# Moving the gather and combination steps of an expert pair out of the w1/w3 products and next to the transposes, in a one-core MoE kernel

## The chip, the cores and the metric

The kernel runs on one core of one Trainium2 chip. The metric is the device time in microseconds (us) of one execution; lower is better.

## The reference, cut to what matters

One encoder block: a mixer (two convolution and state-space branches, not touched here), then a mixture of experts on 512 tokens of width 1024. Each token goes to its two best experts of 64. Everything is float32.

```python
def expert_block(args):
    xblk, e = args
    hdn = jax.nn.silu(xblk @ w1[e]) * (xblk @ w3[e])   # 1024 -> 512
    return hdn @ w2[e]                                  # 512 -> 1024
...
return jnp.zeros_like(xt).at[buf_tok].add(yb * buf_w[:, None])
...
h = h + g2 * moe.reshape(bsz, seq, d)
return _rmsnorm(h, final_g)
```

The tokens of an expert are gathered, go through three weight matrices of 2 MB each, are scaled by their routing weight and are added back to the rows of h that they came from.

## The kernel before

The second half of the program runs over 32 pairs p of experts, two experts e = 0, 1 in a pair, with up to 64 tokens each. The order of instructions is the order of the Python code; TensorE (PE) takes them one after the other, and so do VectorE (DVE), ScalarE (ACT), GpSimd (POOL) and the DMA queue of SyncE (SP).

For one expert, TensorE does:

- `hidden`: the w1 and w3 products, written `ps_w`, for k = 0 to 7, each k with four recorded matmuls of 64 columns of weights (32 in all). ScalarE then applies Silu (tile `sl`) and VectorE multiplies the two halves.
- `hidden_t`: two transposes into `ps_ht`; VectorE copies them out (tile `ht`).
- `second`: the w2 product, written `ps_y`, 16 recorded matmuls of 64 columns of weights.

Two generators supply work for neighbouring pairs, and both use all 128 columns of weights:

- `gather`, letter g: 8 steps a pair, each 12 bf16 matmuls into `ps_g`. They pick the tokens of the *next* pair. After step 4 and after step 8, ScalarE turns what was gathered into four slices each of `xg`, the input of the next pair's `hidden`.
- `combine`, letter c: 8 steps a pair, which add the results of the *previous* pair to h. A step is two matmuls, from `yh` and `yl`, into one `ps_o` tile, and one VectorE addition `h<-h,ps_o` that empties it. The tiles `ps_o` come from the pool `po_` (line 1225), which has two buffers, used in turn: a step can't write before the addition of the step before last has read its buffer.

Between an expert's instructions stand ten places, numbered 0 to 9: 0 to 7 ahead of each k of `hidden`, 8 between `hidden` and the transposes, 9 between the transposes and `second`. A table says which letters stand in which place; `FILL` (line 1375) is that of pairs 3 to 30, 28 pairs, with one row for e = 0 and one for e = 1. What is left of c and g when a pair is done is taken behind `second` of e = 1. Then VectorE builds the one-hot tiles `S` of a later gather (`choose`), and `scale_y` makes `y`, `yh`, `yl` and `so` out of `ps_y` for the next pair's c.

The weights come through a ring of eight 2 MB buffers, named `wb`, whose loads SyncE issues as the products release them.

Of the kernel before, what the change touches and what calls it, by code (L numbers as in the profile page):

```python
# [128 lines left out]
def hybrid_block(ctx: ExitStack, tc: tile.TileContext, a, out, dbg=None, stage=9):  # L129
# [1207 lines left out]
    def combine(ys):  # L1337

        for c in range(4):
            for x in range(2):  # L1340
                yh, yl, st = ys[x][:3]
                if c in sums:
                    ps = sums[c][:, x * T:(x + 1) * T]
                else:
                    ps = pw.tile([P, T], F32, name="ps_o", tag="w") if sums else po_.tile([P, T], F32, name="ps_o", tag="o")
                PE.matmul(ps, lhsT=st[:, c * P:(c + 1) * P], rhs=yh, start=c not in sums, stop=False)
                PE.matmul(ps, lhsT=st[:, c * P:(c + 1) * P], rhs=yl, start=False, stop=True)
                if c not in sums:
                    hv = h[:, c, x * T:(x + 1) * T]
                    V.tensor_add(hv, hv, ps)  # L1350
                yield

    def to_psum():

        pp.close()
        pf = me.enter_context(tc.tile_pool(name="pf", bufs=1, space=PSUM, reuse_waits="tile"))
        for c in range(2):
            ps = pf.tile([P, D], F32, name=f"ps_f{c}", tag=f"f{c}")
            for x in range(2):
                q = slice(x * T, (x + 1) * T)  # L1360
                PE.matmul(ps[:, q], lhsT=ident, rhs=h[:, c, q], start=True, stop=False)
                yield
            sums[c] = ps

    def yps_():
        return [pyy.tile([P, T], F32, name=f"ps_y{x}", tag=f"y{x}") for x in range(2)]
# [5 lines left out]
    FILL1 = [v.split(",") for v in ",,,,g,g,g,g,gg,gg;cx,xc,xc,xc,xc,xc,xc,xc,xc,".split(";")]  # L1372
    FILL2 = [v.split(",") for v in "x,x,x,x,c,c,c,,c,;c,g,gc,g,gc,g,gc,g,g,gc".split(";")]
    FILL3 = [v.split(",") for v in ",c,c,c,c,c,c,c,,;c,,,,,,,,z,z".split(";")]
    FILL = [v.split(",") for v in ",,,,cgcc,,,,gg,gc;,,cgcc,,,,,,gg,gc".split(";")]

    def steps(gen, n):
        for _ in range(n):
# [83 lines left out]
    for p in range(npair):  # L1462
        yps, fl_ = yps_(), FILL3 if p == npair - 1 else (FILL0, FILL1, FILL2, FILL)[min(p, 3)]
        more = {"c": combine(pend) if pend else tb, "g": iter(()), "x": sp_, "G": g0, "z": to_psum()}
# [231 lines left out]
```

## Time and profile before

| | |
|---|---|
| time, median of 3 runs | 1854.08 us (1853.91 to 1859.2) |
| the profiled execution's own time | 1856.45 us |
| its span in the trace | 1854.7 us |
| TensorE busy | 1758.9 us, 95% of the span |
| VectorE busy | 1086.1 us, 59% |
| ScalarE busy | 540.1 us, 29% |
| GpSimd busy | 417.6 us, 23% |
| HBM read | 502.98 MB |

The page gives each engine's busy time over the whole span. Stages have different limits, so the shares alone don't say what a stage waits for; for that the trace is asked for the time of a stage, the waits in it, and the instructions in order of time.

### The profile page before, as it was taken

The numbers are of one execution on the slowest core, as the hardware profiler recorded it, in microseconds if no ns is written. First come the engines' busy times: TensorE is split into PE (matmuls) and PEld (weight loads), VectorE is DVE, ScalarE is ACT, GpSimd is POOL, SyncE is SP. The second block draws the span as 40 slices with busy tenths as digits, with TensorE's granted clock in tenths as the row PEclk, the third lists the DMA queues.
The fourth block names the chain that finished last, engine by engine and source line by source line (L and its number), as shares of the span: only waits on it lengthen the run. The fifth ranks groups of instructions, "written<-read, shape, count | busy, mean of one in ns | idle before, by whom it ended". The sixth has DMA issues, their size and how long they took to land.

```text
span 1854.7 us, 25500 instructions
## 1 busy us (share of the span) xinstructions
PE 1758.9 (95%) x10188; PEld 1048.2 (57%) x10188; DVE 1086.1 (59%) x1728; ACT 540.1 (29%) x901; POOL 417.6 (23%) x288
## 2 busy tenths in 40 slices
PE   5999989989899989999999999999999999999996
PEld 2676767767677878853444444444444444444442
DVE  6789999999989476344334343434343343434344
ACT  2443535425444553433111111111111111111112
POOL 3123341534415454312011111101010101011111
PEclk7999999999999989999999999999999999999998
DMA  6252422524235657568899999999999999999971
GB/s 254 72 162 60 138 89 79 159 69 135 96 111 159 231 203 252 218 247 317 344 386 407 390 406 403 396 405 392 407 389 407 392 405 392 406 389 405 395 319 46
DMA packets 97561, 506.91 MB, mean 273 GB/s; under 512 B 10208, under 2 KB 14560, under 8 KB 51616
## 3 DMA queue, kind: packets, MB, share of 16 engines
q1 hardware_dynamic: 97440, 505.25, 71.0%
q8 instruction: 82, 1.34, 0.3%
q14 instruction: 39, 0.32, 0.1%
HBM read 502.98 MB, written 2.23 MB: 272 GB/s over the span
## 4 chain that ended last, share of the span: by engine, by line
PE 75%; DVE 16%; issue 4%; ACT 2%; DMA 1%; POOL 0%; SPq 0%; DVEq 0%; ACTq 0%; POOLq 0%
PE ps_w L124 24%; PE ps_y L124 13%; PE ps_mm L124 12%; PE ps_g L124 10%; PE ps_o L124 7%; DVE accv L124 4%; DVE w_lo L124 3%; PE ps_cv L124 2%; PE ps_mix L124 2%; PE ps_ys L124 2%; DVE mE L124 2%; DVE ct L124 2%; DVE xs L124 1%; PE ps_ht L124 1%; PE ps_ada L124 1%
## 5 line engine op out<-in xcount | busy, mean ns | idle before, releaser
L124 PE MATMUL ps_w<-wb,xg 128*64 128x512 f32 x2048 | 470.7, 597 | 0.0
L124 DVE TENSOR_TENSOR h<-h,ps_o 128x512 f32<-128x512 f32 x252 | 167.9, 686 | 286.1 <-PE ps_o L124 286.1
L124 PEld LDWEIGHTS ps_w<-wb,xg 128*64 128x64 f32 x2048 | 138.7, 137 | 268.1 <-issue 265.8
L124 PE MATMUL ps_y<-wb,ht 128*64 128x512 f32 x1024 | 236.5, 604 | 2.5 <-DVE ht L124 2.5
L124 PE MATMUL ps_mm<-n1h,w_lo 128*128 128x512 f32 x560 | 224.7, 401 | 10.7 <-DVE w_lo L124 10.7
L124 PE MATMUL ps_mm<-n1h,w_hi 128*128 128x512 f32 x560 | 230.1, 411 | 0.2 <-ACT w_hi L216 0.2
L124 PE MATMUL ps_mm<-n1l,w_hi 128*128 128x512 f32 x560 | 223.2, 398 | 0.0
L124 PE MATMUL ps_g<-S,hg 128*128 128x128 bf16 (+1 forms) x2976 | 210.5, 223 | 1.5 <-DVE S L124 1.5
L124 DVE SCALAR_TENSOR_TENSOR accv<-u,par,accv 128x511 f32<-128x511 f32 (+29 forms) x240 | 206.0, 900 | 6.1 <-ACT accv L437 4.2
L1329 POOL TENSOR_SCALAR so<-par,tabA 128x512 fp32r<-128x512 f32 x32 | 50.0, 1563 | 690.1 <-PE ps_o L124 659.3
L124 PEld LDWEIGHTS <-hg 128*128 128x128 bf16 x2784 | 160.4, 98 | 67.7 <-issue 67.0
L1298 ACT ACTIVATE sl<-ps_w 128x256 f32<-128x256 f32 x64 | 24.6, 384 | 595.5 <-PE ps_w L124 595.5
L124 DVE TENSOR_TENSOR sl<-sl,ps_w 128x256 f32<-128x256 f32 x64 | 39.0, 609 | 259.1 <-ACT sl L1298 259.1
L124 DVE TENSOR_TENSOR w_lo<-w_raw,w_hi 128x1024 fp32r<-128x1024 f32 (+1 forms) x103 | 137.3, 1333 | 81.3 <-ACT w_hi L216 74.0
L216 ACT CAST w_hi<-w_raw 128x1024 fp32r<-128x1024 f32 (+1 forms) x103 | 107.2, 1041 | 266.7 <-PE ps_mm L124 102.7
L124 PEld LDWEIGHTS ps_y<-wb,ht 128*64 128x64 f32 x1024 | 68.6, 138 | 136.8 <-issue 131.2
L1286 ACT ACTIVATE xg<-ps_g,cB,cG 128x128 f32<-128x128 f32 x256 | 96.4, 457 | 144.7 <-PE ps_g L124 144.7
L124 PEld LDWEIGHTS ps_mm<-n1h,w_lo 128*128 128x128 f32 x560 | 108.1, 193 | 39.3 <-DVE w_lo L124 16.0
L124 PEld LDWEIGHTS ps_mm<-n1h,w_hi 128*128 128x128 f32 x560 | 108.2, 193 | 25.9 <-issue 2.4
L124 PEld LDWEIGHTS ps_mm<-n1l,w_hi 128*128 128x128 f32 x560 | 108.6, 194 | 24.4 <-issue 2.2
L124 PE MATMUL ps_o<-yh,so 128*128 128x512 f32 x252 | 117.1, 465 | 2.0 <-DVE h L124 1.3
L844 POOL TENSOR_TENSOR ada_acc<-ada_acc,ada_w 128x512 f32<-128x512 f32 x56 | 89.9, 1607 | 110.6 <-ACT ada_w L842 108.7
(325 smaller groups left out, 2173.2 us busy)
## 6 DMA issues: line engine op xcount, KB each, us to landing
wb<-in_w_dram SPq DMA_DIRECT2D x244, 1024.0 KB, 8.2
wb<-in_w_dram SPq DMA_DIRECT2D x57, 2048.0 KB, 10.0
w_raw<-in_w_in_dram SPq DMA_DIRECT2D x72, 512.0 KB, 3.6
wb<-in_w_dram SPq DMA_DIRECT2D x52, 512.0 KB, 6.9
ada_w<-in_w_ada_dram SPq DMA_DIRECT2D x64, 256.0 KB, 3.6
ada_w<-in_w_ada_dram SPq DMA_DIRECT2D x16, 512.0 KB, 9.1
mE<-sdram SPq DMA_DIRECT2D x32, 256.0 KB, 6.2
w_raw<-in_w_ssm_dram SPq DMA_DIRECT2D x16, 512.0 KB, 3.5
```

What stands on the lines that cost most here:

```text
L124: return f(*args, **kw)
L216: S.copy(hi[:, :n], raw[:, :n])
L844: G.tensor_add(acc, acc, w)
L1286: S.activation(xg[:, q], ps[:, i], AF.Identity, bias=cB2[:, q:q + 1], scale=cG2[:, q:q + 1])
L1298: S.activation(sl, ps[:, 0], AF.Silu)
L1329: G.tensor_scalar(st, tok, tabs2[x][0], None, op0=OP.is_equal)
```

## The change

One line, the table `FILL` of pairs 3 to 30:

```diff
-    FILL = [v.split(",") for v in ",,,,cgcc,,,,gg,gc;,,cgcc,,,,,,gg,gc".split(";")]
+    FILL = [v.split(",") for v in ",,,,,,,,ggc,gccc;,,,,,,,,ggc,gccc".split(";")]
```

Place 4 (e = 0) and place 2 (e = 1) held c g c c and are now empty. Place 8 held g g and holds g g c; place 9 held g c and holds g c c c. That is four c for each expert as before, but three g in place of four: the last two g of a pair go to its end, behind `second` of e = 1.

TensorE in pair 3, e = 0, between the transposes and the w2 product. `ps_o<-yh` and `ps_o<-yl` are one combination step; "waits DVE" marks a matmul that waits for VectorE. Before:

```order
L124 LDWEIGHTS hg
L124 MATMUL ps_g<-S,hg 128x128
L124 MATMUL ps_o<-yh,so 128x512
L124 MATMUL ps_o<-yl,so 128x512
L124 MATMUL ps_y_6669<-wb_5450,ht 64x512 [waits DMAHW2_49,DVE_49]
L124 MATMUL ps_y_6670<-wb_5450,ht 64x512
```

And now:

```order
L124 MATMUL ps_g<-S,hg 128x128
L124 MATMUL ps_o<-yh,so 128x512 [waits Activation_49,Pool_49]
L124 MATMUL ps_o<-yl,so 128x512
L124 MATMUL ps_o<-yh,so 128x512 [waits DVE_49]
L124 MATMUL ps_o<-yl,so 128x512
L124 MATMUL ps_o<-yh,so 128x512 [waits DVE_49]
L124 MATMUL ps_o<-yl,so 128x512
L124 MATMUL ps_y_6669<-wb_5450,ht 64x512 [waits DMAHW2_49,PE_49]
```

Where one combination step stood, three stand in a row, with two waits for VectorE among them.

VectorE in the same stretch, pair 3, both experts (`sl` is the product behind `hidden`, `ht` the copy of the transposes, `h` the addition of a combination step):

```order
-L124 TENSOR_TENSOR h<-h,ps_o 128x512 x3
-L124 TENSOR_TENSOR sl<-sl,ps_w 128x128x2
-L124 COPY ht<-ps_ht 128x256
-L124 TENSOR_TENSOR h<-h,ps_o 128x512 x4
-L124 TENSOR_TENSOR sl<-sl,ps_w 128x128x2
-L124 COPY ht<-ps_ht 128x256
-L124 TENSOR_TENSOR h<-h,ps_o 128x512
+L124 TENSOR_TENSOR sl<-sl,ps_w 128x128x2
+L124 TENSOR_TENSOR h<-h,ps_o 128x512
+L124 COPY ht<-ps_ht 128x256
+L124 TENSOR_TENSOR h<-h,ps_o 128x512 x3
```

The additions that stood ahead of `sl` stand behind it now; one of them is ahead of the copy `ht` and three are behind it. The instructions of POOL and of the DMA queue keep their order.

## Rows read from the trace of the kernel before

**Rows 1.** The page: the span, and the second section's row of TensorE's granted clock, in tenths, over 40 equal slices.

```profile
span 1854.7 us, 25500 instructions
PEclk7999999999999989999999999999999999999998
```

**Rows 2.** Busy times by stretch: pair 2 from its first c on, then pairs 3 to 30. After the stretch and its length: TensorE, weight loads, VectorE, ScalarE, GpSimd busy (with counts), granted clock, DMA share, GB/s.

```profile
880.00:915.50 35.50, 33.67 (x210) 13.39 (x208) 13.40 (x34) 5.02 (x12) 3.13 (x2) 1.00 0.85 323
915.50:1800.30 884.80, 884.80 (x5938) 412.48 (x5936) 349.05 (x691) 140.49 (x336) 87.55 (x56) 1.00 0.98 398
```

**Rows 3.** Waits in the same stretch, pairs 3 to 30: who waited, for whom, us in total, how often, the longest. The two rows are the ones that tell of combination steps; the list has no row in which TensorE waits for another engine or for a DMA.

```profile
DVE h L124 <- PE ps_o L124: 254.4, 168, 5.3
PEld ps_o L124 <- issue: 45.4, 56, 0.8
```

**Rows 4.** TensorE in order of time through one pair of the 28: start, duration (neighbours overlap, so that the distance of two starts is what a group takes), operation, count.

```profile
1199.93 3.60 PE L124 MATMUL ps_w<-wb,xg 128*64 128x512 f32 x16
1203.46 0.49 PE L124 MATMUL ps_o<-yh,so 128*128 128x512 f32 x1
1203.80 0.39 PE L124 MATMUL ps_o<-yl,so 128*128 128x512 f32 x1
1204.03 0.84 PE L124 MATMUL ps_g<-S,hg 128*128 128x128 bf16 x12
1204.68 0.48 PE L124 MATMUL ps_o<-yh,so 128*128 128x512 f32 x1
1204.99 0.40 PE L124 MATMUL ps_o<-yl,so 128*128 128x512 f32 x1
1205.23 0.39 PE L124 MATMUL ps_o<-yh,so 128*128 128x512 f32 x1
1205.46 0.40 PE L124 MATMUL ps_o<-yl,so 128*128 128x512 f32 x1
1205.79 3.65 PE L124 MATMUL ps_w<-wb,xg 128*64 128x512 f32 x16
1209.38 1.51 PE L124 MATMUL ps_g<-S,hg 128*128 128x128 bf16 x24
1210.73 0.39 PE L124 MATMUL ps_ht<-ident,sl 128*128 128x128 f32 x2
1210.95 0.83 PE L124 MATMUL ps_g<-S,hg 128*128 128x128 bf16 x12
1211.59 0.48 PE L124 MATMUL ps_o<-yh,so 128*128 128x512 f32 x1
1211.91 0.40 PE L124 MATMUL ps_o<-yl,so 128*128 128x512 f32 x1
1212.24 3.65 PE L124 MATMUL ps_y<-wb,ht 128*64 128x512 f32 x16
1215.72 1.89 PE L124 MATMUL ps_w<-wb,xg 128*64 128x512 f32 x8
...
1231.53 3.60 PE L124 MATMUL ps_w<-wb,xg 128*64 128x512 f32 x16
```

**Rows 5.** VectorE in order of time in the same pair, e = 0. In brackets: the idle time ahead of it and what ended that.

```profile
1205.43 1.29 DVE L124 TENSOR_TENSOR h<-h,ps_o 128x512 f32<-128x512 f32 x2 [0.52 <-PE ps_o L124]
1209.91 0.61 DVE L124 TENSOR_TENSOR sl<-sl,ps_w 128x256 f32<-128x256 f32 x1 [3.19 <-ACT sl L1298]
1211.15 0.42 DVE L124 COPY ht<-ps_ht 128x256 f32<-128x256 f32 x1 [0.64 <-PE ps_ht L124]
1212.35 0.69 DVE L124 TENSOR_TENSOR h<-h,ps_o 128x512 f32<-128x512 f32 x1 [0.77 <-PE ps_o L124]
```

**Rows 6.** TensorE in order of time in other pairs, which have other tables: a g between two groups of `ps_w` (pair 2), a `ps_y` group with a c behind it and 32 `ps_w` without a break (pair 31).

```profile
895.84 0.84 PE L124 MATMUL ps_g<-S,hg 128*128 128x128 bf16 x12
896.61 1.08 PE L124 MATMUL ps_w<-wb,xg 128*64 128x512 f32 x4
...
1816.31 3.65 PE L124 MATMUL ps_y<-wb,ht 128*64 128x512 f32 x16 [0.52 <-DVE ht L124]
1819.89 0.50 PE L124 MATMUL ps_o<-yh,so 128*128 128x512 f32 x1
1820.56 7.09 PE L124 MATMUL ps_w<-wb,xg 128*64 128x512 f32 x32
1827.57 1.12 PE L124 MATMUL ps_f<-h,ident 128*128 128x512 f32 x2
```

**Rows 7.** All engines in order of time at the end of the program, where four combination steps on two `ps_o` buffers stand in a row: the third, at 1840.05, waits for VectorE's addition of the first.

```profile
1838.04 0.39 PE L124 MATMUL ps_o<-yl,so 128*128 128x512 f32 x1
1838.50 0.40 PE L124 MATMUL ps_o<-yl,so 128*128 128x512 f32 x1
...
1839.31 1.28 DVE L124 TENSOR_TENSOR h<-h,ps_o 128x512 f32<-128x512 f32 x2
...
1840.05 0.19 PEld L124 LDWEIGHTS ps_o<-yh,so 128*128 128x128 f32 x1 [1.58 <-DVE h L124]
1840.05 0.50 PE L124 MATMUL ps_o<-yh,so 128*128 128x512 f32 x1 [1.15 <-DVE h L124]
...
1840.38 0.40 PE L124 MATMUL ps_o<-yl,so 128*128 128x512 f32 x1
```

**Rows 8.** TensorE at the start of pair 31, the first pair behind the 28; its first c stands behind four `ps_w`.

```profile
1802.09 0.47 PE L124 MATMUL ps_o<-yh,so 128*128 128x512 f32 x1 [0.74 <-ACT yh L1327]
```

## The prediction, made before the changed kernel was run

> **What bounds the kernel now.** I read the page first: the granted clock is at or near full from the second slice on [rows 1], so what a matmul takes is the same everywhere that matters here. Then the busy times by stretch. Pairs 3 to 30, the only ones whose table changes, take 884.8 us, and TensorE is busy for all 884.8 of them; VectorE has 349.05 us of work in them [rows 2]. The waits say the same: none of TensorE is listed there, whereas VectorE waits 168 times for a combination step to be done [rows 3]. So the stage is TensorE's list of instructions and the gaps between unlike ones, and a pair takes 1231.53 - 1199.93 = 31.60 us [rows 4]. The DMA engines are close behind: share 0.98 at 398 GB/s [rows 2]. At a full share the same bytes would need about 31.60 x 0.98 = 31.0 us a pair, an estimate from that row, so a faster TensorE could win only 0.6 us a pair before the weights become the limit.
>
> Any microsecond that the new order adds to TensorE's list or opens in it is therefore paid in full: 28 times if it comes once a pair, 56 times if it comes with each expert.
>
> **The change part by part.** The numbers are distances between starts.
>
> *Fewer excursions.* The weight products use 64 columns, g, c and transposes 128, and going over costs something on each side. With c and g away the distance is shorter: the two groups of 16 `ps_w` of e = 0 take 1203.46 - 1199.93 = 3.53 and 1209.38 - 1205.79 = 3.59 us, together 7.12; 32 in one piece behind a c take 1827.57 - 1820.56 = 7.01 [rows 4, 6]. The group of 16 that comes straight from `ps_y` is 0.06 shorter than the one that comes from a c, so for e = 1, which still follows `ps_y` directly, I take 6.95. Before, a pair left the 64-column products four times; now three times, twice around the transposes and once for the two g at its end.
>
> The Trainium skill, page "TensorEngine Tiling (Array Packing)", section "Key Properties", says that a change of tiling mode drains TensorE. By that rule alone, six changes of mode a pair in place of eight, the kernel gets faster by the sum without a wait that is worked out below. The trace agrees that a change costs something: the last `ps_o` takes 0.33 us up to the next `ps_w` where one in a row takes 0.23 [rows 4].
>
> *The new blocks.* Around the transposes an expert now has, in this order: 24 g-matmuls 1.35; yh 0.32; yl 0.24; two transposes 0.22; 12 g-matmuls 0.64; then three c: yh 0.32, yl 0.24, yh 0.23, yl 0.24, yh 0.23, and the last yl up to `ps_y` 0.33 [rows 4]. That is 4.36 us, if nothing waits. How long a yl takes up to a transpose no row shows; it lies between 0.23 (up to a yh) and 0.33 (up to a 64-column product), I take 0.24. The two g at the pair's end: 12 of them between `ps_w` groups take 896.61 - 895.84 = 0.77 [rows 6], 12 more 0.65, so 1.42. A `ps_y` group takes 3.48 where products follow it and 1819.89 - 1816.31 = 3.58 where something with 128 columns does [rows 4, 6].
>
> The pair without a wait: 7.01 + 6.95 + 3.48 + 3.58 + 1.42 + 2 x 4.36 = 31.16 us, which is 0.44 less than 31.60. Over 28 pairs: -12.3 us.
>
> *The new wait.* Three c now stand in a row behind the second g of an expert, with one c ahead of them on the other side of the transposes. They take the two `ps_o` buffers in turn: c1 A, c2 B, c3 A, c4 B. So c4 can't load its weights before VectorE has added c2. I count from c2's yh at 0. Its yl starts at 0.32. VectorE starts an addition 1212.35 - 1211.91 = 0.44 us after the yl has started [rows 4, 5]: at 0.76. TensorE starts on the freed buffer 1840.05 - 1839.31 = 0.74 us after the start of the addition that frees it [rows 7]: at 1.50. Without a wait c4's yh would start at 0.32 + 0.24 + 0.23 + 0.24 = 1.03. So it waits 0.47 us. Then yh to yl is 1840.38 - 1840.05 = 0.33 where a c in a row has 0.23 [rows 4, 7], because the weight load stood behind the wait too. Together 0.57 us an expert, 56 x 0.57 = 31.9 us.
>
> Is VectorE free at 0.76? The addition of c1 is ready at about -0.66 and done by 0.03; the copy `ht`, now behind it, runs till 0.45 (0.42 long [rows 5]). It is free with 0.3 us in hand. c3 needs the addition of c1, long done. What the wait holds up on TensorE is c4 and behind it `second`; ScalarE and POOL have nothing due then. In the old order the two c in a row had c1's buffer and a g of 0.65 between, and the third started at 1205.23 without a gap [rows 4].
>
> Bounds for the wait: 0.47 if the load of c4's weights slips ahead of it; 1.15 + 0.10 = 1.25, the row at the program's end, where VectorE had other work ahead of its addition [rows 7]. No wait at all would need VectorE to be done 0.47 us sooner, and its durations leave no room for that [rows 5]. I take 0.57, since here VectorE is idle when c2 is done.
>
> *What costs nothing.* Silu and product before the transposes: `sl` is done at 1210.52, 1.14 us after `ps_w`, and the transposes come now 1.9 us after it in place of 1.35. The copy `ht` has 12 g-matmuls and three c to hide behind, over 2 us, in place of 1.3. The late two g hold up the second half of `xg`: four ScalarE steps behind the pair's end; the next pair reads those slices at k = 4, half of 7 us later, so they are hidden, and would cost at most their difference if ScalarE were late. The casts `yh` go behind these steps, and the first c that needs them now stands in place 8, over 7 us into the next pair. In pair 31 it does not: its first c stands behind four `ps_w` and already waits 0.74 us for `yh` [rows 8]. There the casts come about 0.8 us later relative to it; +0.8 us, once.
>
> *Sum.* -12.3 + 31.9 + 0.8 = +20.4 us. The profiled execution took 1856.45, which would become 1876.9; it stands 2.4 us above the median of the runs, so from the median 1854.08 I forecast 1874.5 us.
>
> **Rivals.**
>
> *The wait does not come, and the excursions decide (faster).* Place: c4 in place 9. It happens if c2's addition frees its buffer 0.47 us earlier than worked out above. Then -12.3 + 0.8 = -11.5 and 1842.6 us. The wait decides the sign from 11.5 / 56 = 0.21 us an expert on: above, the kernel is slower. For it: VectorE is idle there and TensorE is the only bound. Against: the row in which exactly this wait stands, and 0.44 + 0.74 us from a yl to the freed buffer, against 0.71 that the new order leaves. Chance 0.10.
>
> *The wait is short (no change).* With 0.12 to 0.30 us an expert in place of 0.57 the sum is 56 x 0.12 - 11.5 = -4.8 to 56 x 0.30 - 11.5 = +5.3, so 1849 to 1859 us. It needs VectorE's addition to free the buffer some 0.3 us sooner than the rows of its duration show, and no row has it. Chance 0.07.
>
> *VectorE is late as well (slower still).* If the copy `ht` or c1's addition runs into c2's, each c waits for the one before and the wait goes to the 1.25 us of the program's end [rows 7]: 56 x 1.25 - 12.3 + 0.8 = +58.5, 1912.6 us. Against it the 0.3 us in hand. Chance 0.08.
>
> *The weights are late (slower).* 32 `ps_w` in a piece take 4 MB in 7 us, faster than 398 GB/s bring them [rows 2]; if the ring were nearly empty there, TensorE would wait for a load. For a whole pair the demand falls, and no wait for a DMA is listed today. If it came at half the cost of the c4 wait, 1890 us. Chance 0.05.
>
> The forecast itself: 0.70, between 1866 and 1884 us.
>
> **How the numbers follow.** A measurement of this kernel can tell about 0.3%, 5.6 us. Forecast, late VectorE and late weights are all slower: 0.70 + 0.08 + 0.05 = 0.83. No change 0.07, faster 0.10. The range: the lower bound of the wait (0.47) gives 28 x (0.94 - 0.44) + 0.8 = +14.8, 1868.9; the unknown yl before a transpose adds up to 5 us above; distances between starts that are 0.01 to 0.02 us off, a dozen in a pair, come to about 5 us each way. I give 1863 to 1886, which leaves out the faster rival, most of the late VectorE case and part of the rest, about 2 in 10.
>
> **What would show it.** In the changed trace, in pairs 3 to 30: a pair of about 32.3 us; two waits a pair of `ps_o` for `h` on VectorE, of about half a microsecond idle, 56 in all; 32 `ps_w` in a piece of 7.0 us; 24 g-matmuls of 1.4 us behind `ps_y` of e = 1; the clock still at 1.00, as in pair 2, where TensorE is idle for 1.8 us of 35.5 and the clock is 1.00 [rows 2]; a DMA share of about 0.96. If no wait for `h` is listed there, the prediction is wrong in its main term; if a pair takes 31.2 us plus a wait that differs from 0.57, only its size was.

## The result, and the profile after

The changed kernel takes 1877.28 us (median of 4 runs, 1876.71 to 1879.31). Against the runs of the kernel before, the ratio is 1.0118, with a 95% interval of 1.0101 to 1.0135: slower by 1.2%, or about 22 us (19 to 25). Of the four runs of the kernel before that were taken with it, one took 7382.02 us and is left out; the other three took 1853.91 to 1859.2. The forecast was 1874.5 us, which is +20.4, between 1863 and 1886.

The profiled execution took 1879.31 us. First the stretch that holds pairs 3 to 30, which lie now between 919.0 and 1822.7 us; the first 3.5 us of it still belong to pair 2. The columns are those of [rows 2].

```profile
915.50:1823.50 908.00, 890.23 (x5956) 422.69 (x5956) 343.55 (x702) 133.95 (x336) 88.74 (x56) 1.00 0.98 389
```

Before, TensorE was never idle in these pairs [rows 2]; now it is idle for 17.8 of 908.0 us. The waits of the stretch say for whom, where [rows 3] had no such row:

```profile
DVE h L124 <- PE ps_o L124: 86.6, 168, 0.9
PEld ps_o L124 <- DVE h L124: 42.0, 56, 0.8
PE ps_o L124 <- DVE h L124: 17.7, 56, 0.3
```

56 waits, one for each expert, of TensorE (matmul and weight load) for VectorE's addition `h`. Now one expert of a pair in order of time, TensorE, against [rows 4]:

```profile
1207.99 1.51 PE L124 MATMUL ps_g<-S,hg 128*128 128x128 bf16 x24
1209.44 7.09 PE L124 MATMUL ps_w<-wb,xg 128*64 128x512 f32 x32
1216.46 1.51 PE L124 MATMUL ps_g<-S,hg 128*128 128x128 bf16 x24
1217.78 0.48 PE L124 MATMUL ps_o<-yh,so 128*128 128x512 f32 x1
1218.10 0.40 PE L124 MATMUL ps_o<-yl,so 128*128 128x512 f32 x1
1218.33 0.38 PE L124 MATMUL ps_ht<-ident,sl 128*128 128x128 f32 x2
1218.55 0.83 PE L124 MATMUL ps_g<-S,hg 128*128 128x128 bf16 x12
1219.19 0.48 PE L124 MATMUL ps_o<-yh,so 128*128 128x512 f32 x1
1219.51 0.41 PE L124 MATMUL ps_o<-yl,so 128*128 128x512 f32 x1
1219.75 0.39 PE L124 MATMUL ps_o<-yh,so 128*128 128x512 f32 x1
1219.98 0.40 PE L124 MATMUL ps_o<-yl,so 128*128 128x512 f32 x1
1220.69 0.50 PE L124 MATMUL ps_o<-yh,so 128*128 128x512 f32 x1 [0.32 <-DVE h L124]
1221.03 0.39 PE L124 MATMUL ps_o<-yl,so 128*128 128x512 f32 x1
1221.35 3.65 PE L124 MATMUL ps_y<-wb,ht 128*64 128x512 f32 x16
1224.84 7.04 PE L124 MATMUL ps_w<-wb,xg 128*64 128x512 f32 x32
...
1241.73 7.09 PE L124 MATMUL ps_w<-wb,xg 128*64 128x512 f32 x32
```

And VectorE in the same expert, against [rows 5]:

```profile
1218.53 0.69 DVE L124 TENSOR_TENSOR h<-h,ps_o 128x512 f32<-128x512 f32 x1 [0.94 <-PE ps_o L124]
1219.13 0.42 DVE L124 COPY ht<-ps_ht 128x256 f32<-128x256 f32 x1
1219.95 1.29 DVE L124 TENSOR_TENSOR h<-h,ps_o 128x512 f32<-128x512 f32 x2 [0.40 <-PE ps_o L124]
```

The wait is to be read from the distances. The third c's yl starts at 1219.98; the fourth c's yh would follow 0.24 us later and starts 0.71 later, at 1220.69. So it waited 0.47 us, though the bracket tells only 0.32, which counts from the modelled end of the matmul ahead. Its yl then follows after 0.34 in place of 0.23. A pair, from `ps_w` of e = 0 to the next one, takes 1241.73 - 1209.44 = 32.29 us (32.28 in the mean of the 28); before it was 31.60.

How the span's difference, 1877.6 - 1854.7 = 22.9 us, is made up: the 28 pairs take 903.7 us, from 919.01 to 1822.69, where they took 884.8, from 915.53 to 1800.33: +18.9. Behind them it is 54.9 in place of 54.4: +0.5. The other 3.5 us stand ahead of pair 3, where the two programs are the same. In the traces of the experiments, which have the same instructions there too, pair 3 starts between 912.6 and 918.3; the 919.0 of the changed kernel lies 0.7 us outside. So these 3.5 us are most likely scatter between executions. The +19.4 us that the pairs and the end account for lie within the 19 to 25 of the repeated runs.

### The profile page after: what moved, and what is told of

It is laid out like the page before. It is cut to its first block, busy times and chain, and to the rows that moved or that the text cites. A ratio compares the mean times of both kernels' runs of the same rounds, so it can differ in the third digit from the quotient of the medians.

```text
span 1877.6 us, 25444 instructions
## 1 busy us (share of the span) xinstructions
PE 1760.0 (94%) x10188; PEld 1055.6 (56%) x10188; DVE 1078.5 (57%) x1728; ACT 534.3 (28%) x901; POOL 418.1 (22%) x288
## 4 chain that ended last, share of the span: by engine, by line
PE 71%; DVE 20%; issue 5%; ACT 2%; DMA 1%; POOL 1%; SPq 0%; DVEq 0%; POOLq 0%; ACTq 0%
PE ps_w L124 23%; PE ps_y L124 13%; PE ps_g L124 10%; PE ps_mm L124 9%; PE ps_o L124 6%; DVE accv L124 5%; DVE w_lo L124 3%; PE ps_cv L124 2%; DVE h L124 2%; PE ps_mix L124 2%; DVE ct L124 2%; DVE mE L124 2%; PE ps_ys L124 2%; DVE xs L124 1%; PE ps_ht L124 1%
## 5 line engine op out<-in xcount | busy, mean ns | idle before, releaser
L124 PE MATMUL ps_w<-wb,xg 128*64 128x512 f32 x2048 | 459.7, 596 | 0.0
L124 PE MATMUL ps_g<-S,hg 128*128 128x128 bf16 (+1 forms) x2976 | 205.6, 224 | 1.5 <-DVE S L124 1.5
L124 PEld LDWEIGHTS ps_mm<-n1h,w_lo 128*128 128x128 f32 x560 | 108.1, 193 | 42.3 <-DVE w_lo L124 18.9
```

What stands on the lines that cost most here:

```text
L124: return f(*args, **kw)
```

## The experiments

Three questions: is it the wait of the fourth c, or something else in the new order, such as the two g at the pair's end; do excursions (each time that a pair leaves the 64-column products for work with 128 columns) cost what the distances say; and does the rate of the weights set a floor. All ratios are against the kernel before on the same chip.

**Another buffer, the same order.** In pairs 3 to 30 the last c of each expert writes into the pool of `ps_w` and `ps_ht`. Of the edit, the line that picks the pool, cut:

```diff
-ps = pw.tile(..., tag="w") if sums else po_.tile(..., tag="o")
+ps = pw.tile(..., tag="w") if sums or third and (2 * c + x) % 4 == 3 else po_.tile(..., tag="o")
```

> The changed kernel with its order of instructions untouched; only the last c of each expert in pairs 3 to 30 writes its ps_o into the pool of ps_w and ps_ht, where a buffer is free by then, so that three buffers serve the c in place of two. If the wait of the fourth c for the addition of the second is the cause, it is gone: 31.16 us a pair, 28 x -0.44 + 0.5 = -12 us against the kernel before, a ratio of about 0.994. If the loss comes from the new order itself (the two g at the pair's end, the late xg, the c in a pile), it stays at about +21 us, 1.012.

Measured: 1844.72 us, ratio 0.9939 (0.9919 to 0.9959). TensorE in one expert, e = 1, between the `ps_y` of two e = 0:

```profile
1205.25 3.65 PE L124 MATMUL ps_y<-wb,ht 128*64 128x512 f32 x16
...
1218.44 0.48 PE L124 MATMUL ps_o<-yh,so 128*128 128x512 f32 x1
1218.75 0.39 PE L124 MATMUL ps_o<-yl,so 128*128 128x512 f32 x1
1218.98 0.40 PE L124 MATMUL ps_o<-yh,so 128*128 128x512 f32 x1
1219.22 0.39 PE L124 MATMUL ps_o<-yl,so 128*128 128x512 f32 x1
1219.45 0.39 PE L124 MATMUL ps_o<-yh,so 128*128 128x512 f32 x1
...
1236.36 3.65 PE L124 MATMUL ps_y<-wb,ht 128*64 128x512 f32 x16
```

Three c without a gap: from the first yl on, 0.23 or 0.24 us from one matmul to the next. A pair takes 1236.36 - 1205.25 = 31.11 us, 1.18 less than in the changed kernel, or 0.59 for each expert. With the order of instructions on TensorE unchanged, one more buffer turns a loss of 1.2% into a gain of 0.6%. So the wait for the buffer, with the late weight load behind it, is the whole loss, and the new order itself is worth about half a microsecond a pair.

**Another order, the same buffers.** Place 9 holds c g c c in place of g c c c.

```diff
-    FILL = [... ",,,,,,,,ggc,gccc;,,,,,,,,ggc,gccc" ...]
+    FILL = [... ",,,,,,,,ggc,cgcc;,,,,,,,,ggc,cgcc" ...]
```

> The changed kernel with place 9 holding c g c c in place of g c c c, so that a g of 0.64 us stands between the second c and the last two. No buffer is added. If the wait is the cause it goes (the addition of the second c has 1.4 us): the block around the transposes is 4.44 us in place of 4.36 + 0.57, a pair 31.32, the sum 28 x -0.28 + 0.5 = -7 us, ratio 0.996. If the two g at the pair's end or the empty places 2 and 4 are the cause, nothing changes: 1.012.

Measured: 1849.51 us, ratio 0.9959 (0.9944 to 0.9973); a pair takes 1256.41 - 1225.11 = 31.30 us (forecast 31.32). The g at 1223.26 stands between the second c and the others. TensorE and one weight load (PEld):

```profile
1223.26 0.84 PE L124 MATMUL ps_g<-S,hg 128*128 128x128 bf16 x12
1223.92 0.48 PE L124 MATMUL ps_o<-yh,so 128*128 128x512 f32 x1
1224.23 0.40 PE L124 MATMUL ps_o<-yl,so 128*128 128x512 f32 x1
1224.44 0.19 PEld L124 LDWEIGHTS ps_o<-yh,so 128*128 128x128 f32 x1 [0.25 <-DVE h L124]
1224.46 0.48 PE L124 MATMUL ps_o<-yh,so 128*128 128x512 f32 x1
1224.79 0.40 PE L124 MATMUL ps_o<-yl,so 128*128 128x512 f32 x1
...
1256.41 3.65 PE L124 MATMUL ps_y<-wb,ht 128*64 128x512 f32 x16
```

The fourth c starts 0.23 us after the yl ahead of it: no wait for the buffer is left in the matmuls. A rest of the cost is: its yh takes 0.33, not 0.23, since its weight load still came late, at 1224.44. VectorE's addition of the second c ran from 1223.71 to 1224.39, behind the copy `ht`, and the load waited for it. The two g at the pair's end are still in this kernel, and so are the empty places 2 and 4; neither makes the loss.

**Only the late g.** The kernel before with three g an expert and two at the pair's end, without a third c in a row.

```diff
-    FILL = [... ",,,,cgcc,,,,gg,gc;,,cgcc,,,,,,gg,gc" ...]
+    FILL = [... ",,,,cc,,,,ggc,gc;,,cc,,,,,,ggc,gc" ...]
```

> The kernel before with its excursions kept (c c in places 4 and 2, g g c in place 8, g c in place 9), but with three g an expert, so that two g go to the pair's end as in the changed kernel: five excursions a pair, and no c that waits for a buffer. By the distances: -1.28 for the two g, +1.42 + 0.10 + 0.06 at the pair's end, so +0.30 a pair, 28 x 0.30 + 0.5 = +9 us, ratio 1.005. If the late g, through the late xg and the casts behind it, cause the loss, it is +20 us or more, 1.011.

Measured: 1863.57 us, ratio 1.0042 (1.0026 to 1.0059), which is +8 us; a pair takes 1243.08 - 1211.27 = 31.81 us, 0.21 more than before and 0.09 less than forecast. The late g cost no more than their own fifth excursion.

**One excursion more.** The kernel before with its c g c c split over two places.

```diff
-    FILL = [... ",,,,cgcc,,,,gg,gc;,,cgcc,,,,,,gg,gc" ...]
+    FILL = [... ",,cg,,,cc,,,gg,gc;,,cg,,,cc,,,gg,gc" ...]
```

> The kernel before with one more excursion for each expert: its c g c c is split into c g in place 2 and c c in place 5, so that a pair leaves the 64-column products six times in place of four; no step is added, no c waits for a buffer. By the distances one excursion costs 0.10 (out) + 0.12 (a g up to a product) + 0.06 (in) + 0.03 (a yh behind a product in place of behind a g) = 0.31 us: 56 x 0.31 = +17 us, ratio 1.009. If the gain of the fewer excursions comes from elsewhere, the ratio is 1.000.

Measured: 1882.85 us, ratio 1.0151 (1.0134 to 1.0168), more than expected: +28 us in place of +17. The trace shows the excursions and, beside them, a wait. TensorE at the start of a pair's two experts, e = 0 (from 1205.36 on) and e = 1, and of the next pair:

```profile
1207.18 0.49 PE L124 MATMUL ps_o<-yh,so 128*128 128x512 f32 x1
1207.76 0.49 PE L124 MATMUL ps_o<-yl,so 128*128 128x512 f32 x1
...
1221.80 1.89 PE L124 MATMUL ps_w<-wb,xg 128*64 128x512 f32 x8
1223.62 0.50 PE L124 MATMUL ps_o<-yh,so 128*128 128x512 f32 x1
1223.96 0.40 PE L124 MATMUL ps_o<-yl,so 128*128 128x512 f32 x1
...
1237.90 1.89 PE L124 MATMUL ps_w<-wb,xg 128*64 128x512 f32 x8
```

The expert e = 1, where nothing waits, takes 1237.90 - 1221.80 = 16.10 us; before it took 1231.53 - 1215.72 = 15.81 [rows 4]. So an excursion costs 0.29 us, against 0.31 from the distances. In e = 0 the yl of the first c follows its yh after 0.58 us where e = 1 has 0.34. The list of waits from 915 to 1740 us names the cause:

```profile
PEld ps_o L124 <- DVE yl L124: 10.3, 26, 0.4
```

Place 2 of e = 0 is so early that `yl` of the pair before is not ready. That wait was not in the expectation. With it, 28 x (2 x 0.29 + 0.35) = +26 us, where 0.35 is what the first excursion of e = 0 takes over that of e = 1 (1.70 against 1.35 us from its yh to the next `ps_w`).

**All four in a row.**

```diff
-    FILL = [... ",,,,,,,,ggc,gccc;,,,,,,,,ggc,gccc" ...]
+    FILL = [... ",,,,,,,,gg,gcccc;,,,,,,,,gg,gcccc" ...]
```

> The changed kernel with all four c of an expert in a row: g g in place 8 and g c c c c in place 9. By the wait for two buffers the third c waits 0.47 + 0.10 for the addition of the first, and the fourth, whose addition on VectorE stands 0.65 us behind the first, about 0.09 + 0.10 more: 0.10 us an expert over the changed kernel after what the order saves, +6 us on it, +26 us on the kernel before, ratio 1.014. If each c in a row waited for the one before it, the second and fourth would both wait 0.5 us and more: 1.03.

Measured: 1882.18 us, ratio 1.0146 (1.0127 to 1.0165); a pair takes 1254.58 - 1222.14 = 32.44 us, 0.16 more than in the changed kernel (forecast 0.20).

```profile
1220.17 0.39 PE L124 MATMUL ps_o<-yl,so 128*128 128x512 f32 x1
1220.88 0.50 PE L124 MATMUL ps_o<-yh,so 128*128 128x512 f32 x1 [0.32 <-DVE h L124]
1221.22 0.40 PE L124 MATMUL ps_o<-yl,so 128*128 128x512 f32 x1
1221.48 0.50 PE L124 MATMUL ps_o<-yh,so 128*128 128x512 f32 x1
1221.82 0.40 PE L124 MATMUL ps_o<-yl,so 128*128 128x512 f32 x1
```

Now the third c waits, 0.71 from the yl ahead as in the changed kernel, and the fourth hardly: 0.26 from yl to yh in place of 0.23, and 0.34 to its own yl. The second starts without a wait, so it is not that each c waits for the one before it. With two buffers there is one wait, then VectorE and TensorE are nearly in step; in both c the yl comes 0.34 behind the yh, as where the weight load waited in the changed kernel.

**Everything around the transposes, without a third c in a row.** This run is called `all_in` below.

```diff
-    FILL = [... ",,,,,,,,ggc,gccc;,,,,,,,,ggc,gccc" ...]
+    FILL = [... ",,,,,,,,ggcc,ggcc;,,,,,,,,ggcc,ggcc" ...]
```

> Places 8 and 9 hold g g c c each: all four g and four c of an expert around its transposes, nothing at the pair's end, and no third c without a g ahead of it. Two excursions a pair in place of four. If excursions cost what the distances show: the block is 1.35 + 0.32 + 0.24 + 0.23 + 0.23 + 0.22 + 1.29 + 0.32 + 0.24 + 0.23 + 0.33 = 5.00 us, a pair 2 x (6.95 + 3.48 + 5.00) = 30.86, the sum 28 x -0.74 = -21 us, ratio 0.989. If the weights can't come faster than 406 GB/s (398 at a DMA share of 0.98), the pair stops at 31.0 and TensorE waits for loads of wb: -17 us, 0.991. If excursions cost nothing: about 1.000.

Measured: 1837.96 us, ratio 0.9902 (0.9884 to 0.992). An expert takes 1221.33 - 1205.88 = 15.45, a pair 30.90 us (forecast 30.86), already below the 31.0 that the weights were thought to allow. It is faster than both kernels: two excursions a pair, and no c waits.

**The same with c ahead of g.**

```diff
-    FILL = [... ",,,,,,,,ggc,gccc;,,,,,,,,ggc,gccc" ...]
+    FILL = [... ",,,,,,,,ccgggg,cc;,,,,,,,,ccgggg,cc" ...]
```

> Places 8 and 9 hold c c g g g g and c c: nothing at the pair's end, and no c behind a g; the second pair of c stands behind the transposes, from which a yh follows after 0.13 us in place of 0.22. The block: 0.34 + 0.23 + 0.23 + 0.23 + 2.58 + 0.14 + 0.31 + 0.24 + 0.23 + 0.33 = 4.86 us in place of the 5.0 of all_in, a pair 30.58, 28 x -1.02 = -29 us against the kernel before, ratio 0.985, unless the weights come at 400 GB/s at most: then it stops at about 30.8, like all_in, 0.989.

Measured: 1834.85 us, ratio 0.9893 (0.9878 to 0.9909): a gain as large as that of the last one, and not the larger one expected.

```profile
1216.70 0.50 PE L124 MATMUL ps_o<-yh,so 128*128 128x512 f32 x1
...
1217.74 2.85 PE L124 MATMUL ps_g<-S,hg 128*128 128x128 bf16 x48
1220.43 0.39 PE L124 MATMUL ps_ht<-ident,sl 128*128 128x128 f32 x2
1220.57 0.48 PE L124 MATMUL ps_o<-yh,so 128*128 128x512 f32 x1
...
1221.68 3.65 PE L124 MATMUL ps_y<-wb,ht 128*64 128x512 f32 x16
```

The transposes do take 0.14 up to the next yh, but 48 g-matmuls ahead of them take 2.69 and not 2.58. The block is 4.98 us where 4.86 was expected and 5.0 had been. Why, no run shows. The alternative in the expectation, a floor set by the weights, gave the same number for another reason. In this run's pairs the weights came at 409 GB/s, above the 400 that it assumed, and the next run tells the two apart.

**Does the rate of the weights set a floor?** The table is that of `all_in`, and in pairs 3 to 30 the second matmul of each c is left out.

```diff
-PE.matmul(ps, lhsT=st[...], rhs=yh, start=c not in sums, stop=False)
-PE.matmul(ps, lhsT=st[...], rhs=yl, start=False, stop=True)
+PE.matmul(ps, lhsT=st[...], rhs=yh, start=c not in sums, stop=skip)
+if not skip:
+    PE.matmul(ps, lhsT=st[...], rhs=yl, start=False, stop=True)
```

> Places 8 and 9 hold g g c c each, as in all_in, and in pairs 3 to 30 the second matmul of each c, that from yl, is left out (so the low parts of the results are not added). TensorE's list gets 8 x 0.23 = 1.84 us a pair shorter, from 30.9 to 29.05. If the weights can come faster than 400 GB/s, the pair falls with it: 28 x (29.05 - 31.60) = -71 us against the kernel before, ratio 0.962. If a DMA share of 0.99 means that they can't, the pair stops at about 30.7 and TensorE waits for loads of wb: -25 us, 0.986.

Measured: 1793.16 us, ratio 0.9665 (0.9649 to 0.9681), which is -62 us: most of the -71, but not all. In the first 20 of the 28 pairs an expert takes 1228.99 - 1214.50 = 14.49, so a pair 28.98 us (forecast 29.05). The last eight take 1734.40 - 1493.85 = 240.55, so 30.07 each. Two stretches, columns as in [rows 2], the waits of the later one, and the `ps_y` of e = 1 at either end of the last eight pairs:

```profile
1200.00:1450.00 250.00, 250.00 (x1789) 120.67 (x1788) 111.05 (x223) 43.61 (x105) 28.41 (x18) 1.00 1.01 420
1450.00:1740.00 290.00, 284.21 (x1961) 133.99 (x1960) 119.02 (x236) 49.44 (x119) 31.50 (x20) 1.00 1.01 420
```

```profile
PE ps_w L124 <- DMA wb<-in_w_dram: 4.9, 14, 1.3
```

```profile
1493.85 3.65 PE L124 MATMUL ps_y<-wb,ht 128*64 128x512 f32 x16
...
1734.40 3.65 PE L124 MATMUL ps_y<-wb,ht 128*64 128x512 f32 x16
```

The weights came at 420 GB/s where 398 were moved before at a share of 0.98. Up to 1450 us TensorE never stood still; after that the list has 14 waits for a load, 4.9 us in all, and by the distances the last eight pairs lost 240.55 - 8 x 28.98 = 8.7 us. So here the loads are a little slower than the products, and the stock in the ring lasts for about 20 pairs. Then the loads set the pace. At 398 GB/s a pair of 31.60 us moved 12.6 MB (an estimate from [rows 2] and [rows 4]); at 420 GB/s they need 29.9 us, and the last eight pairs took 30.07. The floor lies at about 30 us a pair, not at 31.0. The two kernels ahead of this one, with 30.9 us, stay above it.

## Why the prediction was right

**The bound.** Right: what the order adds to TensorE's list, and what it opens there, was paid in full. The 28 pairs changed by 18.9 us, which is 0.68 for each (0.70 forecast).

**Fewer excursions.** Right. The pair without the wait was put at 31.16 us; with the third buffer it is 31.11. The 32 `ps_w` take 1216.46 - 1209.44 = 7.02 behind a g and 1231.81 - 1224.84 = 6.97 behind `ps_y` (7.01 and 6.95); the two g at the end 1.45 (1.42); a yl up to the transposes 0.23, the lower of the two bounds. The Trainium skill, page "TensorEngine Tiling (Array Packing)", section "Key Properties", says that a change of tiling mode drains TensorE. The 0.29 us of an added excursion agree with a cost of that kind; no run shows that a drain is the reason. The rival by which only the excursions count is what the kernel with a third buffer shows: 0.994 of the kernel before. It lacked only the buffer.

**The new wait.** Right in place, cause and size: 0.59 us an expert by the kernel with the third buffer, 0.57 forecast. From the second c's yh at 0, the forecast had yl at 0.32, the addition at 0.76, the fourth c at 1.50; the trace has 1219.19, 1219.51, 1219.95, 1220.69, the same three distances. The yh of the fourth c then takes 0.34 (0.33). VectorE was free at 1219.55, 0.40 us ahead of the second c's addition; 0.3 had been reckoned.

**Pair 31.** The direction was right, the size too large: its first c waits 1.18 us for `yh`, where it waited 0.74 [rows 8]; +0.4 and not +0.8.

```profile
1824.95 0.47 PE L124 MATMUL ps_o<-yh,so 128*128 128x512 f32 x1 [1.18 <-ACT yh L1327]
```

**The DMA.** Wrong, and without weight in the sum. The floor of 31.0 us a pair was worked out from a share of 0.98 at 398 GB/s, as if the share were a measure of what is left. In the changed kernel the share is 0.98 at 389 GB/s, not 0.96 as forecast; with c ahead of g it is 1.01 at 409, and without yl 1.01 at 420 GB/s. So the share did not tell how fast the weights could come, and a faster TensorE had about 1.6 us a pair to win, not 0.6.

**The others.** The waits for late VectorE and late weights did not come: `h` and `ht` had their place, and the list of waits of the changed kernel holds three short ones of a product for a load, 1.0 us in all. The late `xg` shows there in 27 weight loads that waited up to 0.3 us for it; the kernel with the third buffer has them too, and its pair is as short as forecast, so they cost nothing. The clock stayed at 1.00 through the pairs.

## What to carry to other kernels

Where one engine has no gap, an order of its instructions can be costed from the distances of starts in its own trace, to a tenth of a microsecond, if every transition is taken from a row that has it: here for the changed kernel and in six of the eight experiments. Two missed by 0.3 us a pair: in one a wait had been overlooked (one more excursion), in the other a long group of g-matmuls had been priced from shorter ones (c ahead of g). Before steps that fill a buffer are put next to each other, count the buffers: with two, the third step in a row waits for whoever empties the first, here 0.47 us plus about 0.1 for the weight load that waited with it. Grouping was right: two in a row with other work between (g g c c, transposes, g g c c) gained 1.0% where three in a row lost 1.2%.

## What the runs showed of the hardware that was not expected

- The DMA engines' busy share was 0.98 at 389 and at 398 GB/s, and 1.01 at 409 and at 420 GB/s: near 1 it didn't tell how much faster the transfers could be.
- A distance between starts depends on both neighbours: a yh behind the transposes came after 0.14 us (c ahead of g) and 0.13 (c g c c), where a g came after 0.22. The 48 g-matmuls in a row took 2.69 us, 0.11 more than reckoned from shorter groups, and the sum stayed nearly the same.
